# A feed-forward block in seven products: hidden rows stored by operand and token quarter, the last group's running sums added on the chip, low parts at the joints on VectorE

## The chip, the core and the metric

One core of a Trainium2 chip runs the whole kernel. The metric is device time in microseconds (us) of one launch; the time of the kernel before is the median of three runs. A profile is one more execution, recorded by the hardware. TensorE (PE in the profile; PEld is its weight load), VectorE (DVE), ScalarE (ACT) and GpSimd (POOL) each work through their own queue in order, and so does the sync engine (SP), whose queue carries nearly all the transfers between HBM and on-chip memory. POOL's queue carries the accumulating ones. All transfers share 16 DMA engines.

## The reference

The kernel computes one layer of a hybrid encoder for 1024 prompt tokens and 64 sample tokens (1088 columns, tokens last). The part that the change touches is the feed-forward block at the end:

```python
h = _rmsnorm(x, p['norm_ffn_w']) @ p['w_up']            # 1024 -> 2 * 2816
ha, hb = jnp.split(h, 2, axis=-1)
hc, ffn_new = _causal_dwconv(ffn_past, ha, p['ffn_conv_w'], p['ffn_conv_b'])
x = x + (jax.nn.silu(hc) * hb) @ p['w_down']            # 2816 -> 1024
```

Before it stand two projections, a state-space scan, attention and the sum of two branches; none of their code is changed.

## The kernel before, in words

Every float32 product is made of three matmuls: both operands are split into a high part (ACT copies the value to a rounded type) and a low part (DVE subtracts the high part from the value), and high x high, high x low and low x high are summed in PSUM.

**The units.** The two feed-forward products are done on 2 x 2 blocks with seven products in place of eight. The four right-hand blocks are b11, b12 (first and second half of the tokens, 544 columns each, for one half of the inner dimension) and b21, b22 (for the other half); t1 to t4 are sums and differences of them. `PARTS` names the seven operands in the order in which they are used: b11, t2, b21, t3, t1, t4, b22. The list `work` has 34 units: 22 of the up product (`pair`, units 0 to 21), then three groups of four of the down product (`pair_down`, units 22 to 25, 26 to 29 and 30 to 33; `DOWN` gives the 8, 8 and 6 row blocks of the hidden layer that a group takes). A unit has 14 steps: for each of seven products p the two quarters s of a half (`QW` = 272 columns). A step is 12 matmuls (9 in the last group) of 128 x 272, which `pile` issues at L1023; its result is taken out of PSUM right after the last of them.

**PSUM.** Products 0 and 2 add into one bank, 1 and 3 into another, 4 and 6 into a third, and 5 has one of its own, each once for every quarter. So product 2 may not start before product 0 has been taken out (L1101, on ACT), 3 waits for 1 (L1103, DVE), and 6 waits for 4 (L1109, DVE). In each case three steps lie between. Seven banks serve in turn.

**Left-hand operands.** While a unit runs, `left_parts` prepares the weights of the next: two loads (L914), four sums on POOL (L918, L919, L929, L936), and for each of seven operands a high part on ACT (L841) and a low part on DVE (L842).

**Up units.** `pair` puts each hidden row block, after convolution, gate and product, into the scratch tensor `h_sc`: 128 rows of 544 columns at a time (L1052). `hidden_sums` reads four such blocks back (L988), makes t1 to t4 of them on POOL (L989 to L992), and writes them to `t_sc` (L994).

**Joints.** A group's right-hand operands are read from these scratch tensors during the unit ahead of the group (units 21, 25 and 29, the joints; `hidden_part`). For each of seven operands and two quarters there are two loads (L1009), each of one or two 272-column pieces per row, which lie apart in memory. Each load takes one of the eight `fb` row buffers, ACT makes the high part (L1010), and the low part (L1011) is made on DVE, except that with s = 1 and j = 2 it is made on POOL.

**Down units.** `pair_down` takes four 128 x 544 results per unit out of PSUM (products 2, 4, 5 and 6; product 2 by ACT at L1105, the others by DVE) and adds each to the output tensor `yT` in HBM by an accumulating transfer issued by POOL (L1092). `yT` holds the residual from before, so three groups add up there.

**What sets the order.** The program is written in the order of the steps above. A planner with a timeline of its own places each instruction on its engine's queue, earlier-written ones first among those that it takes to be ready; waits between engines are put in by the framework from what is read and written.

Of the kernel before, what the change touches and what calls it, by code (L numbers as in the profile page):

```python
# [75 lines left out]
def hybrid_layer(ctx: ExitStack, tc: tile.TileContext, xT, prm, cst, rope, wvd, win, wbs, wba, wout, wup, wdn,  # L76
# [19 lines left out]
    h_sc = scratch("h_sc", [DFF, T])  # L96
    t_sc = scratch("t_sc", [4 * DFF // 2, T // 2])
# [880 lines left out]
    h3 = h_sc.rearrange("(f p) t -> p f t", p=P)  # L978
    t3 = t_sc.rearrange("(k f p) t -> p k f t", k=4, p=P)
    KIND = ("t1", "t2", "t3", "t4")  # L980

    def hidden_sums(i):

        b11, b12, b21, b22 = (row("fb", n)[:, :HALF] for n in ("g11", "g12", "g21", "g22"))
        e = row("fb", "ge")[:, :HALF]
        for u, (x, y) in enumerate(((b11, b12), (b21, b22))):
            for v, t in enumerate((x, y)):
                load(out=t, in_=h3[:, 2 * i + u, HALF * v : HALF * (v + 1)])  # L988
# [4 lines left out]
        for n, t in zip(KIND, (e, b11, b12, b21)):  # L993
            load(out=t3[:, KIND.index(n), i], in_=t)  # L994

    def hidden_part(g, name):

        i0, nk = DOWN_AT[g] // 2, DOWN[g] // 2
        for s in range(2):
            hi, lo = B[name, s] = [unit(*at) for at in home[name, s]]  # L1000
            for j in range(0, nk, 2):
                n = min(2, nk - j)
                t = couple(row("fb", "hr"))[:, :n]
                if name in KIND:
# [4 lines left out]
                load(out=t, in_=src)  # L1009
                S.copy(hi[:, j : j + n], t)  # L1010
                (G if s and j else V).tensor_tensor(out=lo[:, j : j + n], in0=t, in1=hi[:, j : j + n], op=ALU.subtract)  # L1011
# [17 lines left out]
    def pair(f):  # L1029
# [55 lines left out]
    def pair_down(g, j):  # L1085

        u1, u2 = (couple(row("fu", n)) for n in ("u1", "u2"))
        c = {}
        pile = piles(work.index((g, j)), DOWN[g] // 2)

        def put(m, h, t):
            G.dma_start(out=yT[P * m : P * (m + 1), HALF * h : HALF * (h + 1)], in_=t, accum_op=ALU.add)  # L1092

        at = yield
        for _ in range(14):
            p, s = at
            qs = slice(QW * s, QW * (s + 1))
            if s == 0 and p in (2, 4, 5, 6):
# [5 lines left out]
            elif p == 2:  # L1104
                S.copy(c[p][:, qs], pile("a", p, s, False))  # L1105
# [164 lines left out]
```

## Time and profile before

| | us |
|---|---|
| median of 3 runs | 2530.95 (2529.95 to 2533.86) |
| the profiled execution | 2527.61 |
| its span, first to last instruction | 2525.8 |
| TensorE busy in the span | 2440.0 (97%) |
| VectorE busy | 1612.5 (64%) |
| ScalarE busy | 1184.8 (47%) |
| GpSimd busy | 723.2 (29%) |
| first and last matmul of the feed-forward units | about 1774 and 2518 |

A view by windows gives, for each stretch of the span, how long each engine was busy in it, the TensorE clock that was granted, and the share of time that the DMA engines worked. A view of waits gives who waited for whom: the total in us, how often, and the longest. In groups of instructions the columns are: line, engine, operation, tiles written and read, shape and count, then busy time in us and the mean duration in ns of one, then the idle time ahead of them and what ended it.

### The profile page before, as it was taken

The page shows a single profiled execution, that of the slowest core. Times are in us where ns is not written, and L with a number is a line of the kernel's source. Part 1 is how long each engine was busy: PE and PEld are TensorE (multiplying, and loading weights), DVE is VectorE, ACT ScalarE, POOL GpSimd, SP SyncE. Part 2 cuts the span into 40 slices and gives each one's busy share as a digit, 9 for nine tenths or more (in the row PEclk, how much of TensorE's full clock was granted, in tenths as well). Part 3 has the DMA queues.
Part 4 walks back from the last instruction along what each step waited for, and adds up shares of the span by engine and source line. Part 5 has one row for each costly group of instructions (what it writes and reads, how often), then busy time and mean ns, then how long its engine had stood idle before and what let it go on. Part 6 is the DMA issues. An engine that isn't in the chain of part 4 may idle for free. (4 is left out here: it accounts for less than half of the span.)

```text
span 2525.8 us, 44652 instructions
## 1 busy us (share of the span) xinstructions
PE 2440.0 (97%) x16910; PEld 2358.9 (93%) x16910; DVE 1612.5 (64%) x2724; ACT 1184.8 (47%) x2574; POOL 723.2 (29%) x745
## 2 busy tenths in 40 slices
PE   8999999999999999999999998998699999998998
PEld 8999999999999999998889898998699999998998
DVE  6326255854777667447667764645877777786764
ACT  6234243644666455357655754225443434343542
POOL 3000000100111001014433240024476676666543
PEclk9999999999999999999999999999799999999999
DMA  5217158545354354255697745663134333467875
GB/s 165 79 57 275 68 217 246 163 137 152 110 150 138 110 147 117 88 193 175 204 342 240 235 128 198 203 195 107 39 123 140 122 140 120 141 206 185 205 162 97
DMA packets 261911, 399.15 MB, mean 158 GB/s; under 512 B 32288, under 2 KB 190112, under 8 KB 261568
## 3 DMA queue, kind: packets, MB, share of 16 engines
q1 hardware_dynamic: 254784, 382.93, 47.3%
q0 software_dynamic: 6912, 13.37, 3.7%
q8 instruction: 133, 2.18, 0.4%
q14 instruction: 82, 0.67, 0.1%
HBM read 262.65 MB, written 133.56 MB: 157 GB/s over the span
## 5 line engine op out<-in xcount | busy, mean ns | idle before, releaser
L149 PE MATMUL mm<-xn_hi,w_hi 128*128 128x384 f32 (+1 forms) x1416 | 470.3, 332 | 0.9 <-DVE zr L431 0.9
L151 PE MATMUL mm<-xn_hi,w_lo 128*128 128x384 f32 (+1 forms) x1416 | 468.3, 331 | 0.5 <-DVE w_lo L143 0.5
L150 PE MATMUL mm<-xn_lo,w_hi 128*128 128x384 f32 (+1 forms) x1416 | 467.1, 330 | 0.0
L149 PEld LDWEIGHTS mm<-xn_hi,w_hi 128*128 128x128 f32 x1416 | 266.6, 188 | 5.3 <-issue 2.0
L151 PEld LDWEIGHTS mm<-xn_hi,w_lo 128*128 128x128 f32 x1416 | 266.7, 188 | 3.0 <-issue 0.8
L150 PEld LDWEIGHTS mm<-xn_lo,w_hi 128*128 128x128 f32 x1416 | 266.6, 188 | 1.8 <-issue 0.6
L143 DVE TENSOR_TENSOR w_lo<-w_f,w_hi 128x1024 fp32r<-128x1024 f32 (+1 forms) x120 | 152.7, 1273 | 127.6 <-ACT w_hi L142 127.1
L1023 PE MATMUL mx<-n,wh 128*128 128x272 f32 x1156 | 222.0, 290 | 6.2 <-ACT u L1101 2.3
L1023 PE MATMUL mx<-m,w_hi 128*128 128x272 f32 x1114 | 214.4, 290 | 7.0 <-DVE down L1109 5.3
L1023 PEld LDWEIGHTS mx<-n,wh 128*128 128x128 f32 x1156 | 182.8, 190 | 7.3 <-ACT u L1101 2.8
L142 ACT CAST w_hi<-w_f 128x1024 fp32r<-128x1024 f32 (+1 forms) x120 | 125.7, 1049 | 131.2 <-PE mm L150 74.5
L1023 PEld LDWEIGHTS mx<-m,w_hi 128*128 128x128 f32 x1114 | 177.3, 191 | 7.6 <-issue 5.1
L1023 PE MATMUL mx<-n,wl 128*128 128x272 f32 x578 | 167.2, 290 | 0.0
L1023 PE MATMUL mx<-m,w_lo 128*128 128x272 f32 x557 | 161.6, 290 | 0.0
L149 PE MATMUL mm<-b_hi,w_hi 128*128 128x384 f32 (+1 forms) x448 | 147.3, 330 | 6.5 <-DVE b_g L193 3.4
L151 PE MATMUL mm<-b_hi,w_lo 128*128 128x384 f32 (+1 forms) x448 | 146.5, 327 | 0.0
L150 PE MATMUL mm<-b_lo,w_hi 128*128 128x384 f32 (+1 forms) x448 | 146.3, 327 | 0.0
L448 POOL COPY pre<-pre 128x3 f32<-128x3 f32 x48 | 13.1, 273 | 456.3 <-ACT pre L449 332.5
L549 ACT ACTIVATE p_t<-sc,mx 128x1024 f32<-128x1024 f32 (+5 forms) x144 | 106.0, 738 | 76.6 <-DVE mx L540 36.5
L460 DVE SCALAR_TENSOR_TENSOR cc<-pre,par,cc 128x384 f32<-128x384 f32 (+1 forms) x216 | 126.5, 586 | 23.5 <-ACT cc L458 18.4
L841 ACT CAST w_hi<-ws 128x512 fp32r<-128x512 f32 (+1 forms) x68 | 41.4, 608 | 169.6 <-PE mx L1023 122.9
L842 DVE TENSOR_TENSOR wl<-w_f,wh 128x512 fp32r<-128x512 f32 (+1 forms) x102 | 94.7, 928 | 30.3 <-ACT wh L841 29.6
(346 smaller groups left out, 6730.2 us busy)
## 6 DMA issues: line engine op xcount, KB each, us to landing
w_f<-in_win_dram SPq DMA_DIRECT2D x76, 512.0 KB, 3.7
w_f<-in_wup_dram SPq DMA_DIRECT2D x44, 512.0 KB, 3.7
bc<-a_sc SPq DMA_DIRECT2D x32, 512.0 KB, 6.3
out_dram<-down POOLq DMA_DIRECT2D x48, 272.0 KB, 4.9
h_sc<-hb SPq DMA_DIRECT2D x44, 272.0 KB, 2.1
g<-h_sc SPq DMA_DIRECT2D x44, 272.0 KB, 3.7
hr<-t_sc SPq DMA_DIRECT2D x40, 272.0 KB, 4.7
x_sc<-cc SPq DMA_DIRECT2D x48, 192.0 KB, 2.1
```

The lines of the kernel that those rows point to most:

```text
L142: S.copy(hi, w)
L143: V.tensor_tensor(out=lo, in0=w, in1=hi, op=ALU.subtract)
L149: PE.matmul(ps, a_hi, b_hi, start=i == 0, stop=False)
L150: PE.matmul(ps, a_hi, b_lo, start=False, stop=False)
L151: PE.matmul(ps, a_lo, b_hi, start=False, stop=i == n - 1)
L448: G.tensor_copy(pre[:, 0:3], tail)
L460: V.scalar_tensor_tensor(cc[:, :m], pre[:, i : i + m], cw(i), cc[:, :m], ALU.mult, ALU.add)
L549: act(p_t[:n, :nk], sc[c][:n, :nk], AF.Exp, bias=mx[:n, c : c + 1], accum_out=dst)
L841: S.copy(hi, src)
L842: V.tensor_tensor(out=lo, in0=src, in1=hi, op=ALU.subtract)
L1023: PE.matmul(ps, w[x][:, c], b[y][:, k], start=start and k == t == 0, stop=k == nk - 1 and t == 2, skip_group_check=not start)
```

## The change

There are three edits.

1. `h_sc` and `t_sc` become one scratch tensor `q_sc`. Its rows are ordered by operand (b11, b12, b21, b22, t1, t2, t3, t4), then quarter, then partition, and along a row the 11 row-block pairs of 272 columns follow each other. A load of `hidden_part` now reads one piece of up to 544 columns per row. The store of a hidden block, the reads of `hidden_sums` and its writes now move two pieces of 272 columns per row, where they moved one of 544.
2. In the last group the sum with what `yT` holds is made on the chip. Four 128 x 544 blocks of `yT` are loaded (SP queue, `fb` buffers, name `xr`) when the unit begins. Product 2 is taken out by DVE, which adds its block in the same instruction, in place of ACT. POOL adds the block of product 6 to `u2` ahead of time, in two 272-column instructions, and adds those of products 4 and 5 to the finished results, 544 columns each. The results are stored by SP's queue. The first two groups accumulate as before.
3. In `hidden_part` all low parts are made by DVE.

```diff
-    h_sc = scratch("h_sc", [DFF, T])
-    t_sc = scratch("t_sc", [4 * DFF // 2, T // 2])
+    q_sc = scratch("q_sc", [16 * P, DFF // 2 // P * QW])
...
-    h3 = h_sc.rearrange("(f p) t -> p f t", p=P)
-    t3 = t_sc.rearrange("(k f p) t -> p k f t", k=4, p=P)
-    KIND = ("t1", "t2", "t3", "t4")
+    KINDS = ("b11", "b12", "b21", "b22", "t1", "t2", "t3", "t4")
+    q5 = q_sc.rearrange("(n s p) (i t) -> n p s i t", n=8, s=2, t=QW)
+
+    def kind(name):
+        return q5[KINDS.index(name)]
...
-        for u, (x, y) in enumerate(((b11, b12), (b21, b22))):
-            for v, t in enumerate((x, y)):
-                load(out=t, in_=h3[:, 2 * i + u, HALF * v : HALF * (v + 1)])
+        for n, t in zip(first, (b11, b12, b21, b22)):
+            load(out=t, in_=kind(n)[:, :, i])
...
-        for n, t in zip(KIND, (e, b11, b12, b21)):
-            load(out=t3[:, KIND.index(n), i], in_=t)
+        for n, t in zip(KINDS[4:], (e, b11, b12, b21)):
+            load(out=kind(n)[:, :, i], in_=t)
...
-                if name in KIND:
-                    src = t3[:, KIND.index(name), i0 + j : i0 + j + n, QW * s : QW * (s + 1)]
-                else:
-                    f, c = 2 * (i0 + j) + (name[1] == "2"), HALF * (name[2] == "2") + QW * s
-                    src = h3[:, f : f + 2 * n - 1 : 2, c : c + QW]
-                load(out=t, in_=src)
+                load(out=t, in_=kind(name)[:, s, i0 + j : i0 + j + n])
                 S.copy(hi[:, j : j + n], t)
-                (G if s and j else V).tensor_tensor(out=lo[:, j : j + n], in0=t, in1=hi[:, j : j + n], op=ALU.subtract)
+                V.tensor_tensor(out=lo[:, j : j + n], in0=t, in1=hi[:, j : j + n], op=ALU.subtract)
...
-            load(out=h_sc[P * f : P * (f + 1), 544 * h : 544 * (h + 1)], in_=hb[h][:, :544])
+            load(out=kind(("b11", "b12", "b21", "b22")[f % 2 * 2 + h])[:, :, f // 2], in_=couple(hb[h]))
...
+        at_out = {2: (0, 0), 4: (1, 1), 5: (1, 0), 6: (0, 1)}
+        final = g + 1 == len(DOWN)
+
+        def place(p):
+            m, h = at_out[p]
+            return yT[P * (2 * j + m) : P * (2 * j + m + 1), HALF * h : HALF * (h + 1)]
+
+        if final:
+            for p in (2, 6, 4, 5):
+                x[p] = row("fb", "xr")[:, :HALF]
+                load(out=x[p], in_=place(p))
         at = yield
...
             elif p == 2:
-                S.copy(c[p][:, qs], pile("a", p, s, False))
+                ps = pile("a", p, s, False)
+                if final:
+                    V.tensor_tensor(out=c[p][:, qs], in0=ps, in1=x[p][:, qs], op=ALU.add)
+                else:
+                    S.copy(c[p][:, qs], ps)
             elif p == 3:
                 V.tensor_tensor(out=u1[:, s], in0=pile("b", p, s, False), in1=u1[:, s], op=ALU.add)
+                if final:
+                    G.tensor_tensor(out=u2[:, s], in0=u2[:, s], in1=x[6][:, qs], op=ALU.add)
...
-            if s == 1 and p in (2, 4, 5, 6):
-                m, h = {2: (0, 0), 4: (1, 1), 5: (1, 0), 6: (0, 1)}[p]
-                put(2 * j + m, h, c[p])
+            if s == 1 and p in at_out:
+                if not final:
+                    G.dma_start(out=place(p), in_=c[p], accum_op=ALU.add)
+                else:
+                    if p in (4, 5):
+                        G.tensor_tensor(out=c[p], in0=c[p], in1=x[p], op=ALU.add)
+                    load(out=place(p), in_=c[p])
```

More of the change, by code (lines that the diff above doesn't have):

```diff
@@ L1087, in pair_down @@
         u1, u2 = (couple(row("fu", n)) for n in ("u1", "u2"))
-        c = {}
+        c, x = {}, {}
         pile = piles(work.index((g, j)), DOWN[g] // 2)
-        def put(m, h, t):
-            G.dma_start(out=yT[P * m : P * (m + 1), HALF * h : HALF * (h + 1)], in_=t, accum_op=ALU.add)
+        at_out = {2: (0, 0), 4: (1, 1), 5: (1, 0), 6: (0, 1)}
[7 more added lines that the diff above has]
+                load(out=x[p], in_=place(p))
         at = yield
@@ L1097, in pair_down @@
             qs = slice(QW * s, QW * (s + 1))
-            if s == 0 and p in (2, 4, 5, 6):
+            if s == 0 and p in at_out:
                 c[p] = row("fp" if p in (2, 6) else "fh", "down")[:, :HALF]
```

5 lines of the change are left out of this document (3 added, 2 removed).

## The prediction, on record before the changed kernel ran

> **What bounds the kernel now.** I read the page first, then windows around the group changes of the down product, then the waits of the feed-forward block, then single stretches of VectorE's and GpSimd's time, and the end last.
>
> ```profile
> span 2525.8 us, 44652 instructions
> PE 2440.0 (97%) x16910; PEld 2358.9 (93%) x16910; DVE 1612.5 (64%) x2724; ACT 1184.8 (47%) x2574; POOL 723.2 (29%) x745
> ```
>
> TensorE is busy for 97%, and no edit removes a matmul. So only its gaps in the stages that the change touches, and what follows the last matmul, can be won. Windows show the gaps:
>
> ```profile
> core 0: us, PE busy (x) PEld busy (x) DVE busy (x) ACT busy (x) POOL busy (x), PEclk, DMA share, GB/s
> 1830.00:2249.00 419.00, 419.00 (x3343) 418.94 (x3341) 305.13 (x438) 165.53 (x298) 283.38 (x280) 1.00 0.39 135
> 2249.00:2297.00 48.00, 35.94 (x254) 34.65 (x253) 46.94 (x54) 26.28 (x49) 34.03 (x27) 0.93 0.79 237
> 2340.00:2369.00 29.00, 24.80 (x178) 24.59 (x177) 27.79 (x34) 19.25 (x35) 18.11 (x14) 0.88 0.86 235
> 2432.00:2462.00 30.00, 28.14 (x219) 27.39 (x218) 26.19 (x42) 18.60 (x42) 17.38 (x18) 1.00 0.90 224
> 2462.00:2518.00 56.00, 55.93 (x445) 55.71 (x443) 26.58 (x58) 13.97 (x34) 24.22 (x26) 1.00 0.61 100
> ```
>
> In the up units (first row) TensorE never pauses. The three joints follow: it loses 48.00 - 35.94 = 12.1 us, 4.2 and 1.9, in all 18.1, while DVE is busy for 46.94 of 48, 27.79 of 29 and 26.19 of 30 us. The last group (last row) loses nothing, and DVE works less than half of it. So in the joints DVE is the limit. The waits name the instructions:
>
> ```profile
> ACT m L1010 <- DMA hr<-t_sc: 12.6, 12, 2.5
> ACT n L1010 <- DMA hr<-h_sc: 5.8, 5, 2.5
> PE mx L1023 <- DVE down L1109: 5.3, 2, 4.9
> PE mm L1023 <- DVE down L1109: 4.2, 1, 4.2
> PE mx L1023 <- DVE u L1061: 2.4, 1, 2.4
> PE mx L1023 <- ACT u L1101: 2.3, 2, 1.4
> PE mx L1023 <- DVE u L1103: 2.2, 3, 1.1
> PE mx L1023 <- DVE hb L1070: 1.7, 1, 1.7
> ```
>
> The six PE rows add to 18.1: nearly every gap ends when DVE takes a result out of PSUM. Such an instruction is short; it is late because of what stands ahead of it in DVE's queue. ACT also waits for the loads of the joints.
>
> **The change part by part.**
>
> Edit 3, low parts from POOL to DVE. First what a low part costs, and what POOL does to it:
>
> ```profile
> L1011 DVE TENSOR_TENSOR n<-hr,n 128x544 fp32r<-128x544 f32 x10 | 13.0, 1329 | 1.2 <-ACT n L1010 1.2
> L1011 DVE TENSOR_TENSOR m<-hr,m 128x544 fp32r<-128x544 f32 x7 | 4.8, 710 | 0.0
> L1011 POOL TENSOR_TENSOR m<-hr,m 128x544 fp32r<-128x544 f32 x4 | 6.1, 1517 | 3.9 <-ACT m L1010 3.9
> L1011 POOL TENSOR_TENSOR n<-hr,n 128x544 fp32r<-128x544 f32 x2 | 3.5, 1754 | 0.0
> ...
> L1011 POOL TENSOR_TENSOR m<-hr,m 128x272 fp32r<-128x272 f32 x5 | 5.1, 1010 | 2.7 <-ACT m L1010 2.7
> L1011 DVE TENSOR_TENSOR n<-hr,n 128x272 fp32r<-128x272 f32 x4 | 3.3, 825 | 0.0
> L1011 DVE TENSOR_TENSOR m<-hr,m 128x272 fp32r<-128x272 f32 x3 | 1.3, 430 | 0.0
> ...
> 2287.59 4.56 DVE L842 TENSOR_TENSOR wl<-w_f,wh 128x512 fp32r<-128x512 f32 x1
> 2287.45 1.65 POOL L1011 TENSOR_TENSOR m<-hr,m 128x544 fp32r<-128x544 f32 x1
> 2288.76 1.56 POOL L936 TENSOR_TENSOR ws<-w_f,ws 128x512 f32<-128x512 f32 x1
> 2289.98 1.62 POOL L989 TENSOR_TENSOR ge<-g,g 128x544 f32<-128x544 f32 x1
> 2292.07 0.43 DVE L1109 TENSOR_TENSOR down<-mx,u 128x272 f32<-128x272 f32 x1
> ```
>
> The first four rows are of the second joint, the next three of the third, the rest single instructions of the first. The same 544-column low part takes 710 ns in one group and 1329 in another. The 4.56 us instruction, a low part with 512 columns, stood beside three POOL instructions in a row, and the longest gap ended with the L1109 behind it. In that very place one of the three is an L1011 that leaves POOL.
>
> The Trainium skill (SBUF — State Buffer, Who interferes with whom) says that a DVE instruction with two inputs in SBUF and a GpSimd instruction that reads SBUF exclude each other, and that the loser waits for the whole of the other. The trace agrees: 1329 against 710 ns, and 4.56 us beside three. By that rule edit 3 wins, and edit 2 pays for its new POOL sums; both are priced below from rows without it.
>
> There are 7 moved instructions in each joint: 14 of 544 columns, 7 of 272. DVE gains 14 x 0.71 + 7 x 0.43 = 13.0 us of work. Against it stands the delay that goes. A low part behind a POOL instruction is longer by 1329 - 710 = 0.62 us on the mean of a group in which some had no such neighbour; if each of 14 delayed one by a full POOL instruction less some overlap, 1.75 - 0.5 = 1.25. For 272 columns it is 0.40 (825 - 430) to 1.0. Relief: from 14 x 0.62 + 7 x 0.40 = 11.5 to 14 x 1.25 + 7 x 1.0 = 24.5. Net: from +1.5 (slower) to -11.5. I take -4, nearer to the upper end, since the long case above shows that one POOL instruction can cost more than the mean.
>
> A second effect is that row buffers come free sooner. SP holds a load back until the low part that last read its row is done:
>
> ```profile
> SPq L1009 <- POOL m L1011: 5.4, 7, 1.9
> SPq L1009 <- POOL n L1011: 4.6, 4, 1.7
> ```
>
> Eleven loads stood 10.0 us behind POOL. A low part there takes 1.5 to 1.75 us, on DVE 0.71. It is for these loads that ACT waits 12.6 + 5.8 us in the two rows above. The gain lies between 0 and those 18.4; TensorE sees only what is not hidden by its three steps of slack, and I take -1.5.
>
> A third is the clock. These pieces of the chain of waits stand directly behind a gap and further on:
>
> ```profile
> 2361.62 3.08 PE mm L1023 x12
> 2364.71 5.78 PE mx L1023 x36
> 2370.49 3.02 PE mm L1023 x24
> ```
>
> After the gap a matmul takes 257 ns, later 126. The first two pieces cost 8.86 us in place of 48 x 0.126 = 6.0, so 2.8 are lost to the clock, and the windows give 0.88 there and 0.93 in the first joint. If gaps shorten, part of it goes: between 0 and 2.8 + 0.07 x 48 = 6.2; I take -1. The Trainium skill (TensorE: Matmul & The Clock Gate, HAM oscillation — how this bites in real kernels) puts the limit at gaps of more than about 3.4 us. By that rule the whole 2.8 would come back in the second joint as soon as its 4.2 us gap gets under 3.4, and the sum below would be 1.8 us lower.
>
> Edit 1, the layout. Two windows, the first with pieces of 544 columns alone (2176 bytes), the second with 272 (1088 bytes):
>
> ```profile
> DMA packets 348, 0.69 MB, mean 344 GB/s; under 512 B 34, under 2 KB 34, under 8 KB 348
> DMA packets 1025, 1.07 MB, mean 356 GB/s; under 512 B 59, under 2 KB 1024, under 8 KB 1024
> ```
>
> Both were taken with the DMA engines full, and the smaller pieces are not slower. So I cost the edit at nothing, for the joints' loads as for the stores, reads and writes that now have smaller pieces. The latter lie in the up units, where TensorE has no gap, covered by DMA engines at a share of 0.39. Were it gone, POOL's sums would be late, which nothing waits for until the joint. Bounds: 344 to 356 is 3% of the 18.4 us of waits, so +-0.6.
>
> Edit 2, the end. The rows:
>
> ```profile
> 2517.97 0.44 DVE L1113 TENSOR_TENSOR down<-mx,u 128x272 f32<-128x272 f32 x1 [0.69 <-PE mx L1023]
> 2518.70 0.86 POOL L1092 DMA_DIRECT2D out_dram<-down  x1 [1.40 <-DVE down L1113]
> L1266 POOLq DRAIN  x3: 40/102/6389, 2518.7 to 2525.6; - x3
> L1266 SPq EVENT_SEMAPHORE  x11: 17/28/28, 2523.1 to 2525.8; - x11
> DMA to landing us min/median/max: 2.0/2.1/5.2
> ```
>
> The last is of the stores at L1052, of the same size. DVE is done at 2518.41. POOL then issues the accumulating transfer and drains for 6.39 us, to 2525.1; the barrier takes the rest to 2525.8. SP sees the last landing at 2523.1. With the change SP stores right after DVE: 2518.4 + 2.1 = 2520.5, then SP's row of waits (0.6) and the barrier (0.75): 2521.9, a gain of 3.9. Two stores overlap there, so I take -3.7. Bounds: with a landing of 5.2 it is -0.8, with 2.0 it is -4.0.
>
> Edit 2, the four units. Out go 16 POOL transfers of 0.86 us. In come 32 transfers on SP, 8 DVE instructions of 0.44 in place of ACT copies, and on POOL 8 sums of 272 (1.01) and 8 of 544 columns (1.52 to 1.75). POOL's work rises from 24.2 us by at most 8 x 1.01 + 8 x 1.75 - 16 x 0.86 = 8.3, DVE's from 26.6 by 3.5, and each may be held off by the other, 16 x 0.6 to 16 x 1.25 = 10 to 20. At worst DVE has 50 of 56 us. SP issues a store only after the sum that it needs, with the weight loads of the next unit behind it; they wait for their own buffers too. The `xr` loads need rows that the third joint's low parts free, and DVE would stand in its queue for them. Cost: 0, as three steps of 9 matmuls give 27 x 0.126 = 3.4 us of slack, up to 4 units x 1.5 = 6. I take +0.3.
>
> Sum: -4 - 1.5 - 1 + 0 - 3.7 + 0.3 = -9.9. The profiled execution takes 2527.61 us, 1.8 beyond its span, and would take 2517.7. The median of the runs is 3.3 above it; I keep that offset: 2530.95 - 9.9 = **2521.0**.
>
> **Rivals.**
>
> *Only the end is won.* Relief and added work on DVE cancel, as the lower bound has it. For it: POOL has other work in the joints (34.0 us in the first, of which seven L1011 are about 12) that can slide into the time left free. Then -3.7 + 0.3: 2527.5, no measurable change.
>
> *The joints close.* The upper bound of the relief, -11.5, with -3 for the rows and -3 for the clock, and -3.7: about 2510. For it: the gaps add to 18.1 and nearly all end on DVE. Against: the first joint also holds GpSimd's gating and sums.
>
> *DVE is overloaded; slower.* In the joints it is busy for 101 of 107 us. If POOL's other work keeps DVE as slow as now, 13.0 us of new work come on top and every result is taken out later: +13.0 - 3.4 = +9.6, 2540.5. It is slower by 0.2% once less than 4.5 us of the delay goes (13.0 - 3.4 - 5.1). Against it: even the lower bound of the relief is 11.5.
>
> *The new sums in the last group hold up DVE.* Each of 16 POOL sums may hold off a low part as L842 was held off above, with a result behind it. One such delay of 1.5 us beyond the slack in each of 4 units makes 6 us in place of 0.3, and 2521.0 + 5.7 = 2526.7. Against it: DVE is idle for half of that stage. It is what the rule of the Trainium skill (SBUF — State Buffer, Who interferes with whom) would bring where the slack is used up.
>
> **How the numbers follow.** Forecast 42%, only the end 20%, joints close 24%, overloaded 8%, last group 6%. A measurement of this kernel can tell about 0.2%, 5.1 us, from no change. Faster: 42 + 24 = 66%, and 2 of the last group's 6, makes 68%; same: 20 + 4 = 24%; slower: 8%. The range runs from 2508, just beyond the closed joints, to 2532, which leaves out the overload and some of the extremes. The forecast's own range is 2514 to 2526.
>
> **What would show it.** Right: the six PE rows add to 10 to 14 us; the mean of DVE's L1011 in the joints falls towards 710; no POOL L1011; the span ends 3 to 4 us after the last DVE instruction, with a short DRAIN on POOL; no PE gap after 2462. Edit 1 right: the loads' time to landing stays within a few per cent when the DMA engines are full. Wrong: PE waits for L1109 or L1103 in the last group; DVE's L1011 stays at 1.0 us or more; or the planner orders the joints so differently that gaps appear elsewhere.

## The result, and the profile after

| | before | after |
|---|---|---|
| median, same chip, six runs each (us) | 2530.45 (2527.29 to 2537.76) | 2515.89 (2511.01 to 2519.80) |
| ratio of the times, 95% interval | | 0.9937 [0.9920, 0.9955] |
| profiled execution (us) | 2527.61 | 2515.86 |
| its span (us) | 2525.8 | 2514.1 |

The changed kernel is faster by 0.63%, 14.6 us between the medians. The first two lines of its page:

```profile
span 2514.1 us, 44718 instructions
PE 2439.6 (97%) x16910; PEld 2359.5 (94%) x16910; DVE 1609.6 (64%) x2753; ACT 1183.0 (47%) x2566; POOL 703.5 (28%) x724
```

VectorE executes 29 instructions more than before (2753 against 2724: 21 low parts and 8 results of the last group) and is busy for 2.9 us less (1609.6 against 1612.5). That it does more and is busy for less is the main result; the rest of this section shows where this happens.

In the changed code the lines have other numbers: the matmul L1023 is now L1019, the low parts L1011 are L1007, the loads L1009 are L1005, ScalarE's high parts L1010 are L1006, the weights' loads L914 are L913, their four sums on POOL are L917, L918, L928 and L935, their low parts L842 are L841, and the results L1061, L1070, L1101, L1103, L1107, L1109, L1111 and L1113 are L1057, L1066, L1104, L1106, L1114, L1118, L1120 and L1122.

Windows laid from the start of a unit to the start of another, so that they hold the same work in both kernels: units 21 and 22, unit 25, units 29 and 30, units 31 to 33. Before (columns as in the prediction's windows):

```profile
2238.40:2297.10 58.70, 46.64 (x339) 45.30 (x338) 54.13 (x64) 30.23 (x56) 42.28 (x33) 0.94 0.80 244
2339.20:2367.20 28.00, 23.80 (x170) 23.59 (x169) 26.45 (x32) 18.23 (x34) 18.04 (x13) 0.88 0.85 231
2430.50:2470.20 39.70, 37.84 (x296) 37.09 (x295) 32.83 (x55) 22.05 (x50) 23.33 (x23) 1.00 0.82 197
2470.20:2517.90 47.70, 47.70 (x380) 47.51 (x378) 21.04 (x45) 11.13 (x27) 18.81 (x20) 1.00 0.62 100
```

After:

```profile
2244.70:2292.70 48.00, 43.30 (x338) 42.61 (x337) 45.83 (x69) 31.52 (x57) 27.94 (x22) 0.99 0.80 252
2337.30:2359.10 21.80, 21.32 (x170) 21.10 (x169) 20.23 (x29) 14.42 (x27) 8.48 (x6) 1.00 0.83 241
2422.90:2462.50 39.60, 37.60 (x297) 37.10 (x296) 32.28 (x62) 21.53 (x48) 17.25 (x17) 1.00 0.93 263
2462.50:2510.20 47.70, 47.66 (x379) 47.44 (x378) 28.92 (x54) 9.43 (x21) 23.89 (x21) 1.00 0.42 138
```

The first joint shrinks from 58.7 to 48.0 us and the second from 28.0 to 21.8. The third doesn't shrink (39.7 to 39.6), nor do units 31 to 33 (47.7). TensorE does the same number of matmuls in each window; what went is idle time, and some of the slow clock (0.94 to 0.99, 0.88 to 1.00). The four windows together lose 17.0 us; the five units between them take 108.4 us where they took 105.4. Most of that is unit 23, right behind the first window: it takes 23.5 us in place of 21.0, as TensorE's clock is at half there. VectorE's busy time falls by 8.3 and 6.2 us in the two joints that shrink, in the first of them with five instructions more, in the second with three fewer.

The waits after, of TensorE, of ScalarE for the joints' loads, and of the SP queue for row buffers:

```profile
PE mx L1019 <- DVE down L1118: 3.5, 2, 2.1
PE mx L1019 <- DVE hb L1066: 2.0, 1, 2.0
PE mx L1019 <- ACT u L1104: 0.9, 2, 0.5
PE mx L1019 <- DVE u L1114: 0.7, 1, 0.7
PE mm L1019 <- DVE down L1118: 0.5, 1, 0.5
...
ACT m L1006 <- DMA hr<-q_sc: 14.5, 14, 2.7
ACT n L1006 <- DMA hr<-q_sc: 5.5, 7, 1.7
...
SPq L1005 <- DVE n L1007: 23.3, 21, 4.3
SPq L1005 <- DVE m L1007: 15.6, 20, 1.8
```

TensorE's rows add to 7.6 us, where they added to 18.1. For the other engines these are the rows of before that the prediction left out. After the change all the joints' loads come from one tensor, so ScalarE's two rows of after stand against four of before:

```profile
ACT m L1010 <- DMA hr<-h_sc: 2.8, 3, 1.5
ACT n L1010 <- DMA hr<-t_sc: 1.5, 1, 1.5
SPq L1009 <- DVE n L1011: 20.0, 14, 4.3
SPq L1009 <- DVE m L1011: 10.8, 11, 3.5
```

ScalarE's four rows make 12.6 + 5.8 + 2.8 + 1.5 = 22.7 us, against 14.5 + 5.5 = 20.0 after. The loads' waits for low parts make 40.8 us with POOL's 5.4 and 4.6, against 23.3 + 15.6 = 38.9 after. Both are a little shorter; the loads' wait has changed its owner more than its length.

The end, by time, after (SP's and VectorE's instructions; SP's row is of two stores), and then the sequencers' rows at the last line (count, shortest, median and longest in ns, first and last start):

```profile
2509.91 1.16 SPq L1129 DMA_DIRECT2D out_dram<-down  x2
2510.27 0.44 DVE L1122 TENSOR_TENSOR down<-mx,u 128x272 f32<-128x272 f32 x1 [0.70 <-PE mx L1019]
```

```profile
L1279 SPq EVENT_SEMAPHORE  x11: 17/28/28, 2511.1 to 2514.0; - x11
L1279 POOLq DRAIN  x3: 40/102/4102, 2508.5 to 2513.8; - x3
```

VectorE is done at 2510.71 and the span ends at 2514.1, 3.4 us later; before it was 7.4 (2518.41 to 2525.8). From the last matmul's end it is 3.93 against 7.92 us, 4.0 less.

So of the profiled execution: the stretch from the start of unit 21 to the last matmul is 279.5 us before and 265.5 after (-14.0), and the tail is 4.0 us shorter. The stretch begins at 2238.4 before and at 2244.7 after, +6.3. Of this 4.6 us stand ahead of the first matmul of the feed-forward units, where every engine's instructions are the same and in the same order in both; 1.7 us come in units 0 to 20. The start of the stretch lay between 2238.4 and 2248.2 in all the profiled executions of this study, and between 2241.4 and 2245.7 in four executions of one program (below). It is for the most part spread from one execution to the next, and for this reason the experiments below are read by the stretch from unit 21 on beside the median. -14.0 - 4.0 + 6.3 = -11.7 us, the difference of the two profiled executions.

### The profile page after: what moved, and what is told of

It reads as the page before. It is cut to its first block, busy times and chain, and to the rows that moved or that the text cites. A ratio compares the mean times of both kernels' runs of the same rounds, so it can differ in the third digit from the quotient of the medians.

```text
span 2514.1 us, 44718 instructions
## 1 busy us (share of the span) xinstructions
PE 2439.6 (97%) x16910; PEld 2359.5 (94%) x16910; DVE 1609.6 (64%) x2753; ACT 1183.0 (47%) x2566; POOL 703.5 (28%) x724
## 5 line engine op out<-in xcount | busy, mean ns | idle before, releaser
L1019 PE MATMUL mx<-n,wh 128*128 128x272 f32 x1156 | 223.1, 291 | 3.9 <-ACT wh L840 2.3
L1019 PE MATMUL mx<-m,w_hi 128*128 128x272 f32 x1114 | 214.9, 290 | 5.5 <-DVE down L1118 3.5
L1019 PEld LDWEIGHTS mx<-n,wh 128*128 128x128 f32 x1156 | 183.6, 191 | 4.9 <-ACT wh L840 2.7
L1019 PEld LDWEIGHTS mx<-m,w_hi 128*128 128x128 f32 x1114 | 177.3, 191 | 6.2 <-DVE down L1118 4.0
L1019 PE MATMUL mx<-n,wl 128*128 128x272 f32 x578 | 167.3, 290 | 0.0
L1019 PE MATMUL mx<-m,w_lo 128*128 128x272 f32 x557 | 161.8, 290 | 0.0
L686 POOL TENSOR_SCALAR_AFFINE_SELECT bc<-bc 128x1024 f32<-128x1024 f32 (+1 forms) x36 | 39.8, 1106 | 259.6 <-ACT e L673 259.6
```

The source lines that it names most:

```text
L686: G.affine_select(bc[:L, :, :L], bc[:L, :, :L], [[0, 8], [1, L]], ALU.is_ge, -1e30, base=0, channel_multiplier=-1)
L1019: PE.matmul(ps, w[x][:, c], b[y][:, k], start=start and k == t == 0, stop=k == nk - 1 and t == 2, skip_group_check=not start)
```

## The experiments

The theory after the result, A: a POOL instruction that reads SBUF holds off VectorE's instructions with two inputs in SBUF. 21 such POOL instructions left the joints, and what VectorE wins by that is more than their work. Rival B: the joints' loads, whether by the layout or by rows that come free sooner. Rival B': POOL's queue became shorter, and what stands in it came sooner.

All numbers of the trace are of one profiled execution each. "Stage" is from the start of unit 21 to the last matmul's end, "gaps" TensorE's idle time over 0.15 us at a time in it, "half clock" the time in it with a granted clock of 0.5, "tail" from the last matmul to the span's end, "30-33" what the last group takes beyond 4 x 15.83 us.

| run | median us | ratio to before | stage | gaps | half clock | tail | 30-33 |
|---|---|---|---|---|---|---|---|
| before | 2530.45 | | 279.5 | 18.1 | 13.7 | 7.9 | 2.3 |
| after | 2515.89 | 0.9937 [0.9920, 0.9955] | 265.5 | 7.5 | 6.8 | 3.9 | 2.8 |
| layout alone | 2531.64 | 1.0008 [0.9998, 1.0018] | 279.2 | 16.7 | 17.1 | 7.8 | 2.3 |
| end alone | 2528.66 | 0.9992 [0.9982, 1.0002] | 280.9 | 17.5 | 17.1 | 4.2 | 3.0 |
| low parts alone | 2517.04 | 0.9949 [0.9933, 0.9965] | 265.3 | 8.1 | 3.4 | 7.8 | 2.2 |
| without low parts | 2530.11 | 0.9997 [0.9986, 1.0007] | 280.1 | 19.0 | 13.7 | 4.2 | 2.9 |
| POOL reads | 2529.09 | 0.9994 [0.9984, 1.0004] | 279.1 | 17.1 | 17.1 | 3.9 | 2.3 |
| POOL writes | 2517.29 | 0.9949 [0.9930, 0.9967] | 269.1 | 10.2 | 6.8 | 3.9 | 5.7 |
| sums later | 2514.00 | 0.9935 [0.9921, 0.9948] | 265.9 | 8.9 | 3.4 | 3.9 | 3.2 |
| xr spread | 2515.18 | 0.9936 [0.9921, 0.9951] | 264.3 | 7.1 | 3.4 | 3.9 | 1.8 |
| late and spread | 2515.31 | 0.9931 [0.9915, 0.9947] | 265.3 | 9.0 | 0 | 4.0 | 2.6 |
| end as before | 2517.87 | 0.9939 [0.9921, 0.9956] | 262.4 | 6.7 | 0 | 7.6 | 1.5 |
| weight sums on VectorE | 2512.78 | 0.9923 [0.9908, 0.9938] | 263.8 | 7.1 | 0 | 3.9 | 2.2 |
| all sums on VectorE | 2512.47 | 0.9925 [0.9910, 0.9939] | 259.4 | 4.2 | 0 | 4.3 | 3.3 |

Each ratio is to the kernel before as run beside it.

Two things on how to read the table. First, the traces of "after", "sums later", "xr spread" and "late and spread" hold the same instructions on the same tiles in the same order in every queue: the planner undid what the last three had moved in the source. Their rows are four measurements of one program, and they show how far single executions of it spread: the stage from 264.3 to 265.9 us, the gaps from 7.1 to 9.0, the half clock from 0 to 6.8, "30-33" from 1.8 to 3.2. Second, some profiled executions lie at the edge of their runs: those of "end as before" and "all sums on VectorE" are the fastest of six (2510.91 and 2505.45 us), that of "end alone" is the slowest of twelve (2535.11).

### One edit at a time

**Low parts alone.** The kernel before with edit 3 only:

```diff
-                (G if s and j else V).tensor_tensor(out=lo[:, j : j + n], in0=t, in1=hi[:, j : j + n], op=ALU.subtract)
+                V.tensor_tensor(out=lo[:, j : j + n], in0=t, in1=hi[:, j : j + n], op=ALU.subtract)
```

> Only edit 3 on the kernel before: all low parts of the joints on DVE. Theory A: the joints' gaps fall from 18 to 6 to 9 us, the mean of DVE's 128x544 low parts in the second joint from 1075 to below 850 ns, total -10 to -13 us, the end unchanged at 7.9. Theory B: gaps stay at 15 or more, and 13 us of work more on DVE make them no smaller; total within 0.15%.

Measured 0.9949, a stage of 265.3 in place of 279.5 us, and the old tail. One line of code makes the whole gain of the joints. A window over the stage, of this kernel and of the kernel before:

```profile
2242.00:2507.20 265.20, 257.00 (x2017) 254.82 (x2016) 180.04 (x309) 112.70 (x227) 126.69 (x112) 0.99 0.76 188
```

```profile
2238.40:2517.90 279.50, 261.39 (x2018) 258.88 (x2016) 189.88 (x288) 112.60 (x227) 151.60 (x132) 0.98 0.74 177
```

VectorE has 21 instructions more (309 against 288), 13.0 us of work by the prediction's rows, and is busy for 9.8 us less (180.04 against 189.88). So, by that price, 22.8 us of its busy time before was delay, 1.09 us for each low part that left POOL. POOL itself is busy for 24.9 us less (126.69 against 151.60). TensorE's gaps fell by 10.0, as much as VectorE's net gain.

**Layout alone.** Edit 1 only:

```diff
-    h_sc = scratch("h_sc", [DFF, T])
-    t_sc = scratch("t_sc", [4 * DFF // 2, T // 2])
+    q_sc = scratch("q_sc", [16 * P, DFF // 2 // P * QW])
...
-                load(out=t, in_=src)
+                load(out=t, in_=kind(name)[:, s, i0 + j : i0 + j + n])
```

> Only edit 1 of the change on the kernel before: hidden rows stored by operand and quarter. Theory A (delays on DVE by POOL neighbours make the joints' gaps; the layout is worth nothing): TensorE's gaps in units 21 to 30 stay at 18 us within 3, the time from the last matmul to the end stays at 7.9, the total within 0.1% of the kernel before. Theory B (longer pieces land sooner, and this is what closed the joints): gaps at or below 11 us, total -7 or more.

Measured 1.0008 with an interval that holds 1, and the stage as before. The joints' loads of 272 KB land a median of 4.2 us after issue, where those from `t_sc` took 4.7 and those from `h_sc` 3.9. ScalarE waits for the loads for 19.6 us where it waited for 22.7, but the stage is no shorter for it. B by the layout has fallen.

**End alone.** Edit 2 only, `pair_down` as in the diff of the change.

> Only edit 2 on the kernel before: sums of the last group on the chip, stores by SP. Theory A: the time from the last matmul to the end falls from 7.9 to 3.9 us; gaps in units 21 to 29 stay at 17 to 19; unit 30 gets a new gap of about 1.5 us because the loads of the running sums stand ahead of a weight load on SP's queue; total -2 to -3 us. If the end is not bound to the accumulating transfer and POOL's drain, the time after the last matmul stays above 6.

Measured 0.9992 with an interval that holds 1; the medians run side by side are 2.8 us apart (2528.66 against 2531.46), which is what was expected, but not shown. The tail is 3.8 us shorter, and the last group takes 0.7 us more.

**Without the low parts.** The changed kernel with edit 3 undone:

```diff
-                V.tensor_tensor(out=lo[:, j : j + n], in0=t, in1=hi[:, j : j + n], op=ALU.subtract)
+                (G if s and j else V).tensor_tensor(out=lo[:, j : j + n], in0=t, in1=hi[:, j : j + n], op=ALU.subtract)
```

> The changed kernel with the low parts (s = 1, j = 2) back on POOL: edits 1 and 2 alone. Theory A: gaps in units 21 to 30 at 17 to 20 us as before, the end at 3.9; total -2 to -4 us against the kernel before. Theory B: gaps at or below 11, total -11 or more.

Measured 0.9997: with the one line back on POOL the gain is gone. Layout and end together are not to be told from no change.

### What in POOL's low parts cost the time

Both kernels put idle work on POOL at the 21 places that the low parts left, and leave everything else of the changed kernel as it is. It goes to 256 columns of a tile of constants that nothing reads any more. In the first every instruction reads SBUF. The second reads two columns at each place, in one copy, and otherwise only writes:

```diff
                 V.tensor_tensor(out=lo[:, j : j + n], in0=t, in1=hi[:, j : j + n], op=ALU.subtract)
+                [G.tensor_tensor(out=con[:, :256], in0=con[:, :256], in1=hi[:, j + k, :256], op=ALU.subtract)
+                 for k in range(n if s and j else 0)]
```

```diff
                 V.tensor_tensor(out=lo[:, j : j + n], in0=t, in1=hi[:, j : j + n], op=ALU.subtract)
+                [G.tensor_copy(con[:, :2], hi[:, j, :2]) if k == 0 else G.memset(con[:, :256], 0.0)
+                 for k in range(1 + 3 * n if s and j else 0)]
```

> The changed kernel, with idle work on POOL: at each of the 21 places from which a low part left POOL, POOL subtracts 256 columns of the new high part from a dead constant tile, twice where the low part had 544 columns, once where it had 272. VectorE keeps all low parts. No output depends on the tile. Theory A (a POOL instruction that reads SBUF holds off VectorE's two-input instructions, and that was the loss): the mean of VectorE's L1007 with 544 columns rises from 0.78 to 0.84 us to between 1.0 and 1.4, the stretch from unit 21 to the last matmul from 265.4 us to between 273 and 285, the time to between 2523 and 2535 us. Rival B (what was won is that rows come free sooner and that nothing waits for POOL's low parts; neighbours don't matter): L1007 stays at 0.8 us and the time at 2516 +- 3.

> The same with idle work that reads almost nothing: at each of the 21 places a copy of 2 columns of the high part, then memsets of 256 columns of the dead tile, six where the low part had 544 columns, three where it had 272, to keep POOL busy about as long. Theory A: L1007 stays at 0.8 us on the mean and the time near that of the changed kernel, 2514 to 2520 us. Rival B': it is not reading that counts but that POOL's queue is long, so that its sums, gates and transfers come late: the time rises here about as much as with the reading work, to 2523 us or more, while L1007 stays short in both. Rival B: 2516 +- 3 in both.

The windows over the stage, of the changed kernel, with reading idle work, with writing idle work:

```profile
2244.70:2510.20 265.50, 257.92 (x2018) 256.07 (x2016) 187.66 (x317) 110.38 (x219) 130.00 (x112) 0.99 0.73 203
```

```profile
2243.50:2522.60 279.10, 261.82 (x2018) 258.92 (x2016) 206.23 (x317) 110.16 (x219) 167.03 (x148) 0.97 0.72 194
```

```profile
2242.50:2511.60 269.10, 258.80 (x2018) 256.43 (x2016) 188.65 (x317) 110.14 (x219) 176.43 (x239) 0.99 0.73 201
```

The same 317 instructions take VectorE 187.66, 206.23 and 188.65 us. 37 us of POOL work that reads gives 18.6 us back to VectorE's delay, 13.6 us to the stage and the time of the kernel before (0.9994). That is more POOL time than the low parts had taken (24.9 us), so the amounts are not to be compared one by one. 46 us of POOL work that writes gives 1.0 and 3.6 us; 2.9 of the latter stand in the last group, where a gap of 2.3 us in unit 30 is followed by half clock for 3.4 us. So it is the reading that made the loss. A longer queue on POOL costs at most these 3.6 us, and whose low part frees a row decides nothing: A stands, B and B' have fallen.

Which instructions are held off, from groups by shape from 2240 to 2470 us, which holds the joints. With reading idle work:

```profile
L1007 DVE TENSOR_TENSOR m<-hr,m 128x544 fp32r<-128x544 f32 x40 | 38.1, 973 | 0.2 <-ACT m L1006 0.2
L1007 DVE TENSOR_TENSOR n<-hr,n 128x544 fp32r<-128x544 f32 x30 | 32.1, 1097 | 5.6 <-ACT n L1006 4.3 <-DMA w_f<-in_wdn_dram 1.2
L841 DVE TENSOR_TENSOR wl<-w_f,wh 128x512 fp32r<-128x512 f32 x24 | 25.3, 1053 | 8.5 <-ACT wh L840 8.2
...
L1118 DVE TENSOR_TENSOR down<-mx,u 128x272 f32<-128x272 f32 x12 | 5.1, 432 | 2.4 <-PE mx L1019 2.4
```

In the changed kernel:

```profile
L1007 DVE TENSOR_TENSOR m<-hr,m 128x544 fp32r<-128x544 f32 x40 | 32.3, 826 | 2.5 <-ACT m L1006 2.5
L1007 DVE TENSOR_TENSOR n<-hr,n 128x544 fp32r<-128x544 f32 x30 | 26.5, 910 | 4.5 <-ACT n L1006 4.4
L841 DVE TENSOR_TENSOR wl<-w_f,wh 128x512 fp32r<-128x512 f32 x24 | 21.7, 903 | 9.2 <-ACT wh L840 8.8
...
L1118 DVE TENSOR_TENSOR down<-mx,u 128x272 f32<-128x272 f32 x13 | 5.6, 434 | 2.6 <-PE mx L1019 2.6
```

With writing idle work:

```profile
L1007 DVE TENSOR_TENSOR m<-hr,m 128x544 fp32r<-128x544 f32 x40 | 31.1, 797 | 2.8 <-ACT m L1006 2.8
L1007 DVE TENSOR_TENSOR n<-hr,n 128x544 fp32r<-128x544 f32 x30 | 29.3, 1007 | 5.4 <-ACT n L1006 5.4
```

A low part has both inputs in SBUF. Beside reading idle work it grows from 826 to 973 and from 910 to 1097 ns, and one of the weights (L841) from 903 to 1053. The expectation had 1.0 to 1.4 us; the two groups of L1007 together have 1.00 (70.2 us by 70), its lower edge. In the changed kernel they have 0.84 (58.8 us), and beside writing idle work 0.86 (60.4 us). L1118, with one input in PSUM and one in SBUF, takes 434 and 432 ns: it isn't touched. A result that is taken out late is late by what stands ahead of it in VectorE's queue. The Trainium skill (SBUF — State Buffer, Who interferes with whom) says all of this for VectorE's tensor_tensor instructions, which all of these are: VectorE contends with a GpSimd instruction that reads SBUF, not with one that only writes it, and only where two of VectorE's inputs lie in SBUF. The runs agree on each of the three, by 18.6 us against 1.0, and by 434 against 432 ns.

### What is left in the changed kernel

**Hidden sums of the last pair later.**

```diff
-                if p == 3 and i < FT + 2 and i % 2 == 0:
+                if p == 3 and i < FT and i % 2 == 0:
                     hidden_sums(i // 2 - 1)
+                if p == 3 and i == FT + 2:
+                    hidden_sums(FT // 2 - 1)
```

> The changed kernel, with the hidden sums of the last pair (four 544-column POOL instructions with their loads and stores) emitted after product 3 of the third unit behind the joint and not of the second. If POOL neighbours are what is left of the loss in the first joint, the gaps of units 21 to 23 fall from 8.3 us to about 5 and the time to about 2512 us. If VectorE's own work is the bound there, the gaps stay at 8 us and the time at 2516 us; if the later sums hold up the second joint's loads, it rises by 1 to 3 us.

Measured 0.9935, a stage of 265.9 us, and units 21 to 23 lose 8.3 us as in the changed kernel. This says nothing about the question, because nothing moved. (In the source the sums stood in unit 22, the first unit behind the joint and not the second.) On POOL the first of them, L990, begins right behind the weight sum L935 in both traces, at 2291.13 us in the changed kernel and at 2289.29 here, and the whole program is that of the changed kernel. Whether these four instructions make a part of the gaps stays open. The changed kernel's trace shows a candidate: ahead of the late L1118, VectorE's L841 begins at 2290.06 us and takes 1.65 us, where the two of its shape ahead of it take 0.67 and 0.68, beside POOL's L935 and L990.

**Loads of the running sums spread.** First the gap that they were suspected of, in unit 30 of the changed kernel (SP's, POOL's and VectorE's time):

```profile
2445.40 0.82 SPq L1096 DMA_DIRECT2D xr<-out_dram  x2
2447.04 0.33 SPq L913 DMA_DIRECT2D w_f<-in_wdn_dram  x1
2448.02 3.66 SPq L1096 DMA_DIRECT2D xr<-out_dram  x6
...
2453.83 1.02 POOL L917 TENSOR_TENSOR ws<-w_f 128x384 f32<-128x384 f32 x1 [2.99 <-DMA w_f<-in_wdn_dram]
...
2457.14 0.82 DVE L841 TENSOR_TENSOR wl<-ws,wh 128x384 fp32r<-128x384 f32 x1 [4.14 <-ACT wh L840]
```

The weight load L913 stands among the loads of edit 2 in SP's queue. POOL waits for it for 2.99 us, then ScalarE for POOL and VectorE for ScalarE, and a gap of TensorE of 1.5 us, which L1118 ends, closes at 2460.1. The experiment was to be

```diff
-            for p in (2, 6, 4, 5):
-                x[p] = row("fb", "xr")[:, :HALF]
-                load(out=x[p], in_=place(p))
...
+            if final and s == 0 and p in (0, 1, 2, 3):
+                u = (2, 6, 4, 5)[p]
+                x[u] = row("fb", "xr")[:, :HALF]
+                load(out=x[u], in_=place(u))
```

> The changed kernel, with the four loads of the running sums in each unit of the last group issued one each at products 0 to 3 and not all ahead of product 0. If these loads, ahead of the weight load in SP's queue, made the 1.5 us gap in unit 30, that gap goes, the loss of units 30 to 33 falls from 2.8 us to about 1 and the time to about 2514 us. If the gap has another cause, nothing changes (2516 us). If the loads now come too late for VectorE's sums, TensorE waits for L1106 or L1118 in units 30 to 33 and the time rises by 1 to 4 us.

Here the gap on L1118 is 0.4 us, the last group takes 1.8 us beyond its matmuls, and the median is 2515.18. But the program is again that of the changed kernel: in SP's queue L913 still stands between the first two of these loads and the next six. The gap was 1.5, 1.5, 0.4 and 0.9 us in four executions of it ("after", "sums later", "xr spread", "late and spread"). So it varies by itself, and that the loads of edit 2 make it is read from one trace and not tested.

**Both together.** The two diffs above in one kernel.

> The changed kernel with both small moves together: the last pair's hidden sums after product 3 of the third unit behind the joint, and the loads of the running sums one each at products 0 to 3. If the moves add, the gap in unit 30 is below 0.6 us as with the spread loads alone and the time is 2511 to 2514 us; if what showed for either alone was within the spread of single executions, it is 2514 to 2517 us.

Measured 2515.31 (0.9931), the gap 0.9 us, and the same program once more. What the three kernels give is the spread: with "after" they are 23 runs of one program between 2509.32 and 2520.74 us, with medians from 2514.00 to 2515.89 and ratios from 0.9931 to 0.9937.

**End as before.** The changed kernel with `pair_down` as it was, so layout and low parts alone.

> The changed kernel without the new end: layout and low parts as changed, the last group's outputs again by accumulating transfers of POOL. If the new end is worth its 3.85 us of tail against 0.5 to 1.5 us of new gaps in the last group, the tail is 7.8 us, the loss of units 30 to 33 about 2 us in place of 2.8, and the time 2 to 4 us above that of the changed kernel, 2517 to 2520 us. If the new sums and loads of the last group cost as much as the end wins, it is 2514 to 2517 us.

Measured 2517.87, 0.9939 [0.9921, 0.9956], where the changed kernel has 0.9937 [0.9920, 0.9955]. In this execution, the fastest of its six, the tail is 3.7 us longer than after the whole change, the last group 1.3 us shorter (0.3 to 1.7 by the four executions), and the stage 3.1 us shorter (1.9 to 3.5). Whether edit 2 is worth anything beside edit 3 stays open: the tail shows 3.6 to 4.0 us in every pair of profiles that differ in the end, the medians differ by 2.0, and the intervals hold a difference of either sign.

**The trade carried on.** 12 weight sums, those of the first unit of each group, on VectorE; then all 48 of the down units and the four hidden sums of the last pair. The diff is of the first; the other three sums are changed like the one shown, and the second kernel has `V` for every unit:

```diff
-    def left_parts(blocks):
+    def left_parts(blocks, E=G):
...
-        G.tensor_tensor(out=s1, in0=q21, in1=q22, op=ALU.add)
+        E.tensor_tensor(out=s1, in0=q21, in1=q22, op=ALU.add)
...
-        return left_parts([wdn[:, o + n * m : o + n * (m + 1)] for m in (2 * f, 2 * f + 1)])
+        return left_parts([wdn[:, o + n * m : o + n * (m + 1)] for m in (2 * f, 2 * f + 1)], V if f == 0 else G)
```

> The changed kernel, with the four sums of weights (512 columns, L917, L918, L928, L935) of the first unit of each down group on VectorE and not on POOL: 12 instructions, all in or near the joints, all with two inputs in SBUF. If the trade of the low parts holds on (21 moved instructions shortened the stage by 14 us, 0.67 each), 12 more would be worth up to 8 us; no more than the 7.5 us of gaps and 6.8 us of halved clock that are left: time between 2508 and 2513 us. Rival: with 47 of 48 us busy in the first joint VectorE is at its own limit, 12 x 0.7 = 8.4 us more work there is not won back, and the time is the same or up to 6 us longer (2516 to 2522).

> The changed kernel, with all 48 weight sums of the twelve down units on VectorE, and the four hidden sums of the last pair too: of POOL's two-input work in the joints only the gates are left. If every such instruction next to low parts costs more on POOL than on VectorE, also with VectorE busy for 90% of the joints, the time is below that of the 12 moved weight sums, 2508 to 2512 us. If VectorE's own work is the bound by now (52 x 0.7 = 36 us more of it between unit 21 and the end, in which it is busy for 201 of 295 us), or its queue makes results come late where POOL did not stand in the way, the gaps of units 21 to 33 rise above 7.5 us and the time is 2514 to 2522 us.

Windows over the stage, of the first and of the second:

```profile
2242.20:2506.10 263.90, 256.59 (x2018) 253.57 (x2016) 186.74 (x329) 109.92 (x219) 114.82 (x101) 1.00 0.74 206
```

```profile
2239.90:2499.30 259.40, 255.06 (x2018) 253.35 (x2016) 195.61 (x369) 110.59 (x219) 60.77 (x60) 1.00 0.74 208
```

Twelve more instructions cost VectorE nothing that shows: 186.74 us, where the four executions of the changed kernel have 186.2 to 187.7. 52 more cost it 8.0 us over the changed kernel, 0.15 each for work of about 0.7. The first stage, 263.8 us, is not to be told from the 264.3 to 265.9 of the changed kernel. The second, 259.4 us with gaps of 4.2, lies below all four, though it was taken from the fastest of its six runs. So the rival (VectorE at its own limit) has fallen for the second kernel, as far as the stage goes. That the second would be faster than the first was not met: their medians are 2512.47 and 2512.78. Their ratios, 0.9925 and 0.9923, lie below the 0.9931 to 0.9937 of the changed kernel, but the intervals (0.9910 to 0.9939 and 0.9908 to 0.9938, against 0.9920 to 0.9955 of "after") overlap, so that they beat it is likely and not shown. Both are surely faster than the kernel before.

## Why the prediction was right, and where not

It gave 2521.0 us (2508 to 2532), faster. The time was 2515.89: the sign and the mechanism of the largest term were right, and the gain was 14.6 us between the medians where 9.9 were forecast. Of its signs, POOL has no low part left, the span ends 3.4 us after VectorE, and no gap lies behind 2462. The six rows of TensorE were to add to 10 to 14 us and add to 7.6. VectorE's low parts of 544 columns take 0.84 us, neither near the 0.71 that was to show it right nor at the 1.0 that was to show it wrong.

**Relief of VectorE: right, mis-sized.** This is the step that failed in size: -4 net, that is 17 us of relief against 13.0 of work. Low parts alone shows 22.8 us of relief and 9.8 net, near the bound that the prediction worked out from a full POOL instruction per low part (24.5). The prediction calls its choice nearer to the upper end; it is not. 17 us lie a little below the middle of 11.5 to 24.5 (18.0), and the lower end is a mean over a group (0.62 us) in which some instructions had no neighbour on POOL. The row of one long case (4.56 us beside three POOL instructions) was the better guide. The ends were also counted by the moved instructions alone, while the weights' low parts are held off too (903 ns, and 1053 beside reading idle work).

**Rows free sooner, -1.5: wrong as a step.** Its bound of 18.4 us was two of four rows; ScalarE waited for these loads for 22.7. Low parts alone shows the step by itself: SP's waits for low parts fall from 40.8 to 34.8 us, so rows do come free sooner, but ScalarE waits for the loads for 23.8 us and not less. That its 1.5 us made up for a part of what the relief lacked is luck. POOL reads shows that the gain goes where this step would still have held: there the low parts stay on VectorE, and the time is that of before.

**Clock, -1: mis-sized.** The half clock fell from 13.7 to 6.8 us in the stage. At half speed that is 3.4 us of matmuls, within the bound of 6.2. Gaps (10.6) and clock (3.4) make the 14.0 us of the stage. In the other three executions of the program the half clock was 3.4, 3.4 and 0 us, so the size of this term differs from one execution to the next. In the second joint the 4.2 us gap was followed by 6.8 us of half clock before; now the gap is 0.5 us and the clock 1.00 throughout. The rule of the Trainium skill that the prediction quoted (TensorE: Matmul & The Clock Gate, HAM oscillation — how this bites in real kernels) agrees with that; in the first joint it does not, see below.

**Layout, 0: right.** 1.0008 [0.9998, 1.0018], and the stage as long as before (279.2 against 279.5 us).

**End, -3.7: right for the tail.** It is 4.0 us shorter; that the whole launch is shorter by it stays open (end alone, end as before). A detail was wrong: POOL's DRAIN is not short but takes 4.10 us. It begins at 2508.5, when POOL's last sum is in hand, and ends at 2512.6, before SP's last wait, so it hides. Before, it began after the last transfer's issue at 2518.7.

**Last group, +0.3: not contradicted, with a detail wrong.** TensorE waits for L1118 in unit 30 (0.4 to 1.5 us in four executions), which the prediction named as a sign against it. Its trace leads to weight loads among the new transfers in SP's queue; the prediction had named weight loads behind the new stores, and its bound of 6 us covers the wait. The last group takes 1.8 to 3.2 us beyond its matmuls in the four executions of the changed program, 2.9 and 3.0 in end alone and without low parts, and 1.5 to 2.3 with the old end (before, layout alone, low parts alone, end as before). The means differ by 0.6 us, and the ranges overlap. VectorE's busy time in the stage rises from 180.04 us in low parts alone to 187.66 after the whole change, 4.1 more than the 3.5 of its 8 new instructions. That fits the delay by the new sums on POOL that the prediction named, but was not tested by itself. In units 31 to 33 VectorE had the room (28.92 of 47.7 us).

**The rivals.** *Only the end is won* and *overloaded* have fallen with the run of edit 3 alone. The time lies between the forecast and *the joints close* (2510), whose bound of the relief was nearly met. But the joints didn't close: 7.5 us of gaps are left. *The new sums hold up VectorE* had 6 us where the last group as a whole lost at most 3.2.

## What to carry to other kernels

Where VectorE is busy for most of a stretch, the POOL instructions beside it that read SBUF are not free: the 21 low parts, 24.9 us of POOL's time, cost VectorE about 22.8 us here, 37 us of idle reading 18.6, and giving VectorE the work of the low parts as well (13 us) still made it less busy. To price such a move, compare one VectorE shape with and without a POOL neighbour and count every two-input instruction of the stretch, not only the moved ones. A test that separates causes is cheap: put the suspected neighbour back as idle work, once as reads and once as writes. And before a moved statement is called without effect, the trace has to show that it moved: three edits here left every queue as it was.

## What was not expected of the hardware

The clock was halved after gaps of two microseconds, and not each time. Two gaps of about 2 us in the first joint of the changed kernel, and what follows each:

```profile
2263.00:2265.10 2.10, 0.15 (x2) 0.00 (x0) 2.10 (x6) 0.79 (x2) 0.00 (x0) 1.00 0.89 239
2265.10:2268.50 3.40, 3.36 (x26) 3.36 (x27) 3.40 (x6) 2.69 (x5) 0.00 (x0) 1.00 0.84 281
2290.00:2292.10 2.10, 0.06 (x1) 0.00 (x0) 2.10 (x4) 0.00 (x0) 2.10 (x2) 0.83 0.36 133
2292.10:2298.20 6.10, 6.08 (x27) 6.08 (x28) 2.89 (x7) 0.39 (x1) 4.86 (x5) 0.50 0.92 231
```

After the first, 26 matmuls take 3.4 us at full clock; after the second, 27 take 6.1 us at 0.50. The four executions of this program show that it isn't settled by the gap's length or by what the program does there:

| | first gap | half clock behind it | second gap | half clock behind it |
|---|---|---|---|---|
| after | 2.0 us | 0 | 2.1 us | 6.8 us |
| sums later | 2.0 | 0 | 2.1 | 3.4 |
| xr spread | 2.0 | 3.4 | 1.5 | 0 |
| late and spread | 1.9 | 0 | 2.1 | 0 |

A gap of 0.7 us stands ahead of the second one in three of the four, "late and spread" among them, so it doesn't decide it either. Wherever the clock was halved in the stage, in all of these traces, it stayed so for 3.4 or 6.8 us at a time. The Trainium skill (TensorE: Matmul & The Clock Gate, HAM oscillation — how this bites in real kernels) speaks of gaps over about 3.4 us; here gaps of 2.0 and 2.1 us were enough in some executions and not in others, and the measurement decides. What follows is that a short gap may cost more than its own length again (6.8 us at half speed are 3.4 us lost), and that of two executions of one program one may pay it and the other not.

VectorE's total can fall when work is added to it: 21 instructions more and 9.8 us less busy time in the stage (low parts alone), where they came from POOL.
